# A decoder step on one core: another order and another split of x in the opening

## The chip, the cores and the metric

The kernel runs on one core of a Trainium2 chip. The metric is the device time of one execution in microseconds; the median of three runs stands for a kernel. Engines are named as in the profile: PE is TensorE (PEld its weight loads), ACT ScalarE, DVE VectorE, POOL GpSimd, SP SyncE, which issues most of the transfers.

## The reference

One layer over 1024 prompt tokens and 8 sample tokens, with 1024 features. The part in question is the beginning:

```python
xn = _rmsnorm(h, pre_g)                              # x * rsqrt(mean(x*x) + eps) * gain
proj = jnp.einsum('bld,de->ble', xn, w_in)           # 1024 -> 7168 columns
u, v, z_a, x_b, z_b, g_a, g_b = jnp.split(proj, SPLITS, axis=-1)
...
e = jnp.einsum('blp,pd->bld', p, w_ple)              # embedding, 256 -> 1024, used at the very end
gate = jax.nn.sigmoid(jnp.einsum('bld,de->ble', _rmsnorm(h, ple_in_g), w_pg))
h = h + _rmsnorm(gate * e, ple_out_g)
```

Everything is float32, and the products must be close to float32 in precision.

## The kernel before

**Products.** A float32 operand is split into a high and a low part (`split`: ACT copies to the rounded type `F32R`, DVE subtracts that from the source). A product is three matmuls for each block of 128 features: high by high, high (weights) by low (x), low (weights) by high (x). The normalised x lies in SBUF with features on partitions, in `big`: eight blocks `k` of 128 features, and tokens along the row. `quarter(kp, j)` is the pair of blocks 2kp and 2kp+1 on half `j` of the tokens (512 each; half 1 also has the 8 sample tokens, `[:, :, HALF:]`). B11 and B21 are features 0 to 511 and 512 to 1023 of half 0, B12 and B22 the same of half 1. `xop` holds their high and low parts, as two tiles for each `kp`.

Most products of the kernel use Strassen's seven, on sums (T1 to T4) of these quarters, which are made in place in `big` (`combine`); so `big` must hold the whole values of x. The first pair of v columns goes the plain way (`classical`), with four steps: `steps[0]` is A11 by B11 plus A12 by B21, `steps[1]` A21 by B11 plus A22 by B21, and `steps[2]` and `steps[3]` the same on half 1. Each step's `prepare` splits its weights (128x512 each; `vw`), `run` puts 24 matmuls (48 on half 1) into one PSUM region, `evacuate` copies it out on ACT.

**PSUM.** There are three regions of two banks (`region`) and two single banks (`bank`); each new one takes the place of one that is done with, and PE waits until that has been read.

**Order.** Each engine takes its instructions strictly in the order of its queue. Up to `steps[2]` and the embedding of tile 6, the order on every queue is that of the calls in `begin()`. After that a planner sets the order by estimated times and due times (`Planner.order`), starting from the estimated state at the end of the opening.

**The opening.** `begin()` issues all early loads on SP: p (256 features of the embedding input) and its weights first, then x tiles 0 to 3, the sample rows, the weights of v, x tiles 4 to 7, the second half of p. Until p lands, PE transposes the identity into `warm`. Then:

- `p_turn(h, q)` turns two tiles of p by four transposes and splits them; `we.cut` splits the embedding's weights.
- `embed(t)` multiplies the embedding of token tile t (12 matmuls into a region) and `embed_out` copies it to SBUF (ACT, or DVE for tile 0) and stores it.
- `norm_root(t)` squares x tile t on ACT with a sum, DVE adds epsilon (`ms`), POOL raises to -0.5 (`rstd`); `norm_scale(t)` multiplies the tile on DVE. `S` is the sample's tile `xe`.
- `x_half(j, kps)` turns x: for each `kp` eight transposes of 128x128 into a region (`pst`), copied with the gain to `big` on DVE for even and on ACT for odd `kp`. `x_extra` does it for the sample (eight small transposes `pxe`, four DVE multiplications). `xop.cut` then splits a quarter from `big`.

Before the change, `begin()` has `x_half(0, (0, 1, 2))`, `x_extra`, `xop.cut("B11")`, `x_half(0, (3,))`, `embed(3)`, `xop.cut("B21")` and `steps[0].run()`; the roots of tiles 4 to 7 stand behind that, and half 1 is turned behind `steps[1].run()`, followed by its cuts and `embed(4)`, `embed(5)` and `steps[2].run()`.

Of the kernel before, what the change touches and what calls it, by code (L numbers as in the profile page):

```python
# [12 lines left out]
AF = mybir.ActivationFunctionType  # L13
ALU = mybir.AluOpType
# [291 lines left out]
def hybrid_step(  # L306
# [103 lines left out]
    def quarter(kp, j):  # L410
        both = big[:, 2 * kp : 2 * kp + 2, :].rearrange("p a t -> p (a t)")
        return (both[:, 2 * HALF :] if j else both[:, : 2 * HALF]).rearrange("p (k t) -> p k t", k=2)
# [170 lines left out]
            t = 2 * self.pair + m  # L583
            return big[:, 4 * k : 4 * k + 4, t * P : (t + 1) * P]

    def product(form, ps, weights, operand, what, first, last, again=False):

        plan.apart()
        wide = what not in ("B11", "B21", "T4")
        for k in range(4):  # L590
            (wh, wl), (xh, xl) = weights, operand.at(what, k)
            for i, (w, x) in enumerate(((wh, xh), (wh, xl), (wl, xh))):
                for o, c in form.pieces(ps, wide):
                    nc.tensor.matmul(o, w[:, k, :], x[:, c],
                                     start=first and k == 0 and i == 0, stop=last and k == 3 and i == 2,
                                     skip_group_check=again)

    def halves(t, j):

# [9 lines left out]
    def classical(weights, operand, user):  # L609

        steps, regions = [], {}
        for j in range(2):
            for m in range(2):
                names = [f"A{m + 1}{k + 1}" for k in range(2)]

                def prepare(names=names):
                    for n in names:
                        if n not in weights.ready:
                            weights.prepare(n)

                def run(names=names, j=j, m=m):
                    ps = regions[m, j] = region("acc")
                    for i, n in enumerate(names):
                        product(Features, ps, weights.ready[n], operand, f"B{i + 1}{j + 1}", i == 0, i == 1)

                def evacuate(j=j, m=m):
                    user.direct(m, j, Features.view(regions[m, j], j == 1))

                steps.append(Step(prepare, run, evacuate))
        steps[0].loads = lambda: (weights.fetch(), user.loads())  # L630
        steps[-1].after.append(user.finish)
        return steps
# [194 lines left out]

    col = lambda i, k: gvec[:, i * NB + k : i * NB + k + 1]

    def x_half(j, kps):  # L830

        for kp in kps:
            ps = region("pst")
            for kk in range(2):
                k = 2 * kp + kk
                for i in range(4):
                    nc.tensor.transpose(ps[:, kk, i * P : (i + 1) * P],
                                        xts[4 * j + i][:, k * P : (k + 1) * P], ident)
            out = quarter(kp, j)[:, :, :HALF]
            for kk in range(2):  # L840
                o, i, gain = out[:, kk], ps[:, kk], col(0, 2 * kp + kk)
                if kp % 2:
                    nc.scalar.activation(out=o, in_=i, func=AF.Copy, scale=gain)
                else:
                    nc.vector.tensor_scalar_mul(o, i, gain)

    def x_extra():
        ps = bank("pxe").rearrange("p (k t) -> p k t", k=NB)
# [366 lines left out]
    def pairs_of(c0, cls, key):  # L1215
        return [(Weights(inp(c0, i), key), cls(i, key)) for i in range(NPAIR)]
# [2 lines left out]
        step.after.append(f)  # L1219


    vsteps, vusers = [], []
    for i, (w, u) in enumerate(pairs_of(V0, V, "v")):
        vsteps.append((strassen if i else classical)(w, xop, u))
        vusers.append(u)
    gasteps = [strassen(w, xop, u) for w, u in pairs_of(GA0, Gate, "ga")]
    usteps = []
    zausers = []
# [369 lines left out]

    def embed_terms(t, n, terms):

        if t not in e_ps:
            e_ps[t] = region("e")
        todo = left.setdefault((t, n), 6)
        for k, (i, j) in terms:
            nc.tensor.matmul(e_ps[t][:, n], pcut[t // 4][i][:, k, t % 4 * P : (t % 4 + 1) * P], we.at(n, k)[j],
                             start=todo == 6, stop=todo == 1)
            todo -= 1
        left[t, n] = todo

    def embed(t):  # L1610
        for n in range(2):
            embed_terms(t, n, [(0, HH), (0, HL), (0, LH), (1, HH), (1, HL), (1, LH)])

    def embed_out(t, by=None):
        e = slot("e", (P, 2, HALF))
        if by is None:
            nc.scalar.activation(out=e, in_=e_ps.pop(t), func=AF.Copy)
        else:
            nc.vector.tensor_copy(e, e_ps.pop(t))
        r = t // 2 * 2 * P  # L1620
        dma(kept["e"][r : r + 2 * P].rearrange("(p i) (n c) -> i p n c", i=2, n=2)[t % 2], e)

# [7 lines left out]
    def begin():  # L1630
        psl = slot("psamp", (P, PLE))
        p_load(0, 0)
        for i, v in enumerate((pre_g, pool_scale, ple_in_g)):
            dma(vecs[i * NB : (i + 1) * NB, :], v[0].rearrange("(k p) -> k p", p=P), nc.scalar)
        we.fetch(0)
        p_load(0, 1)
        we.fetch(1)
        for t in range(4):
            x_load(t)
        dma(xe[:NS], x_sample)  # L1640
        steps[0].loads()
        for t in range(4, NB):
            x_load(t)
        for q in range(2):
            p_load(1, q)
        dma(psl[:NS], p_sample)
        praw.append(psl)
        steps[4].loads()
        fetched[0] = 5
        early_loads()  # L1650

        ps = bank("warm")
        for t in range(12):
            nc.tensor.transpose(ps[:, t % 4 * P : (t % 4 + 1) * P], ident, ident)
        p_turn(0, 0)
        we.cut(0, 0)
        we.cut(0, 1)
        ps = bank("warm")
        for t in range(4):
            nc.tensor.transpose(ps[:, t * P : (t + 1) * P], ident, ident)  # L1660
        p_turn(0, 1)
        for k in range(2):
            for t in range(2):
                embed_terms(t, 0, [(k, HH)])
            for t in range(2):
                embed_terms(t, 0, [(k, LH)])
        for t in range(2):
            embed_terms(t, 0, [(0, HL), (1, HL)])
        we.cut(1, 0)
        we.cut(1, 1)  # L1670
        for t in range(2):
            embed_terms(t, 1, [(0, HH), (0, LH), (1, HH), (1, LH), (0, HL), (1, HL)])
        norm_root(0)
        embed_out(0, nc.vector)
        norm_root(1)
        norm_scale(0)
        embed(2)
        norm_root(2)
        norm_scale(1)
        norm_root(3)  # L1680
        norm_scale(2)
        embed_out(1)
        norm_scale(3)
        norm_root(S)
        vps = bank("vecs")
        nc.tensor.transpose(vps[:, : 3 * NB], vecs[: 3 * NB, :], ident[: 3 * NB, : 3 * NB])
        nc.vector.tensor_copy(gvec, vps[:, : 3 * NB])
        embed_out(2)
        norm_scale(S)
        steps[0].prepare()  # L1690
        x_half(0, (0, 1, 2))
        x_extra()
        xop.cut("B11")
        x_half(0, (3,))
        embed(3)
        xop.cut("B21")
        steps[0].run()
        embed_out(3)
        norm_root(4)
        norm_root(5)  # L1700
        norm_scale(4)
        steps[1].prepare()
        norm_scale(5)
        norm_root(6)
        norm_root(7)
        norm_scale(6)
        norm_scale(7)
        steps[0].evacuate()
        steps[1].run()
        x_half(1, (0, 1))  # L1710
        for q in range(2):
            p_turn(1, q)
        x_half(1, (2, 3))
        steps[1].evacuate()
        xop.cut("B12")
        embed(4)
        xop.cut("B22")
        embed_out(4)
        embed(5)
        embed_out(5)  # L1720
        prepared[0] = 4
        steps[2].run()
        steps[2].evacuate()
        embed(6)
        embed_out(6)
# [47 lines left out]
```

## Time and profile before

| | us |
|---|---|
| three runs | 991.76, 990.98, 991.16 |
| their median | 991.16 |
| the profiled execution | 991.0 |
| its span, first to last instruction | 989.3 |

The profile is of one execution. Its page gives the busy time of each engine, and the timeline the start, the length and, in brackets, the idle time ahead of an instruction and what ended it. A PE row's length is modelled; matmuls overlap, so their starts tell the pace. Several equal instructions in a row are one line, with their count.

### The profile page before, as it was taken

Reading aid. Unit: us, or ns where it says so; the run is one execution under the profiler, and the core shown is the slowest. Engines: PE = TensorE matmul, PEld = TensorE weight load, DVE = VectorE, ACT = ScalarE, POOL = GpSimd, SP = SyncE. Lnnn points to the kernel's source line nnn. Section 1 sums busy time; section 2 is a strip of 40 time slices with the busy share of each in tenths; the row PEclk is TensorE's granted clock in tenths of the full one; section 3 lists DMA queues with packets and bytes.
Section 4 is the critical chain, followed back from the end, with each engine's and each line's share of the span. In section 5 each row is a group of like instructions: output and inputs, shape, how many; then the busy total and the mean of one; then the engine's idle time right before and its main releaser. Section 6 shows DMA issues by size and latency. Waiting matters only on the chain. (4 is left out here: it accounts for less than half of the span.)

```text
span 989.3 us, 15945 instructions
## 1 busy us (share of the span) xinstructions
PE 975.0 (99%) x6087; PEld 875.3 (88%) x6087; DVE 797.4 (81%) x1239; ACT 529.6 (54%) x888; POOL 69.9 (7%) x142
## 2 busy tenths in 40 slices
PE   8999999999999999999999999999999999999996
PEld 7789999999998999999999999999999988888885
DVE  6796568787769888979897987697799899779696
ACT  7778987565434433344442333562353365877463
POOL 2100001000000000000000100000000001313111
PEclk9999999999999999999999999999999999999999
DMA  9335553322374354556735075973663552699546
GB/s 339 132 104 117 120 151 128 129 85 75 120 256 149 125 202 142 215 197 213 255 124 191 17 268 207 315 281 131 228 244 124 177 191 63 133 299 361 149 109 191
DMA packets 109291, 174.53 MB, mean 176 GB/s; under 512 B 28632, under 2 KB 68016, under 8 KB 109207
## 3 DMA queue, kind: packets, MB, share of 16 engines
q1 hardware_dynamic: 107118, 166.13, 49.1%
q0 software_dynamic: 2048, 7.37, 4.4%
q8 instruction: 48, 0.79, 0.3%
q14 instruction: 29, 0.23, 0.1%
q10 hardware_dynamic: 48, 0.01, 0.0%
HBM read 114.84 MB, written 53.87 MB: 171 GB/s over the span
## 5 line engine op out<-in xcount | busy, mean ns | idle before, releaser
L299 DVE TENSOR_TENSOR u<-acc,u 128x520 f32<-128x520 f32 (+1 forms) x90 | 62.6, 696 | 37.3 <-PE acc L299 33.5
L299 POOL TENSOR_TENSOR rstd<-ms,mhalf 128x1 f32<-128x1 f32 (+1 forms) x36 | 32.3, 900 | 193.5 <-DVE ms L299 183.8
L299 POOL MEMSET u<- 128x8 f32 x35 | 4.0, 150 | 499.9 <-PE acc L299 235.8
L299 ACT ACTIVATE u<-acc 128x512 f32<-128x512 f32 x39 | 23.2, 595 | 25.6 <-PE acc L299 25.0
L299 ACT ACTIVATE paw<-pas 128x512 fp32r<-128x512 f32 x16 | 10.1, 629 | 30.0 <-DVE pas L299 24.8
L299 ACT ACTIVATE pbw<-pbs 128x512 fp32r<-128x512 f32 x16 | 10.0, 628 | 28.0 <-DVE pbs L299 24.8
L299 DVE TENSOR_TENSOR big<-big 128x1024 f32<-128x1024 f32 (+4 forms) x20 | 23.6, 1218 | 0.0
L299 ACT ACTIVATE big<-mix 128x256 f32<-128x256 f32 x32 | 12.1, 383 | 19.1 <-PE mix L299 16.8
L299 PE MATMUL accm<-qh,wpoolw 128*128 128x260 f32 (+1 forms) x96 | 20.9, 319 | 0.0
L299 ACT ACT_TABLE_LOAD x13 | 16.7, 1283 | 7.2 <-PE acc L299 6.2
L299 ACT ACTIVATE big<-v 128x1024 uint16<-128x1024 uint16 x16 | 18.5, 1175 | 3.8 <-DMA v<-vw 3.8
L299 ACT ACTIVATE zbw<-zbs 128x512 fp32r<-128x512 f32 x16 | 10.1, 628 | 16.7 <-DVE zbs L299 11.8
L299 DVE TENSOR_TENSOR v<-acc,u 128x520 f32<-128x520 f32 (+1 forms) x9 | 6.3, 697 | 15.4 <-PE acc L299 15.4
L299 DVE TENSOR_TENSOR acc<-acc,u 128x512 f32<-128x512 f32 (+1 forms) x16 | 11.2, 699 | 8.7 <-PE acc L299 8.7
L299 ACT ACTIVATE gbw<-gbs 128x512 fp32r<-128x512 f32 x16 | 10.0, 626 | 15.0 <-DVE gbs L299 12.8
L299 ACT ACTIVATE zaw<-zas 128x512 fp32r<-128x512 f32 x16 | 10.0, 630 | 14.6 <-DVE zas L299 9.1
L299 ACT ACTIVATE uw<-us 128x512 fp32r<-128x512 f32 x16 | 10.0, 626 | 13.7 <-DVE us L299 11.1
L299 PEld LDWEIGHTS accm<-qh,wpoolw 128*128 128x128 f32 x96 | 15.6, 188 | 1.9
L299 DVE TENSOR_TENSOR big<-mix,big 128x256 f32<-128x256 f32 x32 | 12.7, 420 | 5.5 <-ACT big L299 5.1
L299 ACT ACTIVATE gb<-gb 128x1032 f32<-128x1032 f32 (+1 forms) x8 | 6.8, 854 | 19.0 <-DVE gb L299 19.0
L299 ACT ACTIVATE vw<-v 128x1024 uint16<-128x1024 uint16 x16 | 16.1, 1046 | 0.5 <-DVE v L299 0.5
L299 ACT ACTIVATE big<-h 128x1024 f32<-128x1024 f32 (+1 forms) x12 | 13.0, 1092 | 5.0 <-DMA h<-in_x_prompt_dram 5.0
(690 smaller groups left out, 3623.5 us busy)
## 6 DMA issues: line engine op xcount, KB each, us to landing
ga<-ga SPq DMA_DIRECT2D x16, 516.0 KB
gb<-gb SPq DMA_DIRECT2D x16, 516.0 KB
ya<-za SPq DMA_DIRECT2D x8, 516.0 KB
yb<-zb SPq DMA_DIRECT2D x8, 516.0 KB
x<-in_x_prompt_dram SPq DMA_DIRECT2D x8, 512.0 KB
vraw<-in_w_in_dram SPq DMA_DIRECT2D x8, 512.0 KB
e<-e SPq DMA_DIRECT2D x8, 512.0 KB
garaw<-in_w_in_dram SPq DMA_DIRECT2D x8, 512.0 KB
```

The source lines that it names most:

```text
L299: getattr(getattr(self.nc, e), method)(*args, **kwargs)
```

## The change

The opening is put in another order, and x is split in another way.

- *Fillers:* seven in place of twelve before p, six in place of four after its first turn. The first four embedding matmuls come ahead of p's second turn.
- *Embedding:* tile 3 is multiplied ahead of x, into two single banks, and copied out by DVE; tile 0's copy by DVE comes after the root of tile 2.
- *The split of x:* for each `kp`, ACT copies the two blocks from PSUM with the gain to the high part, and DVE makes the low part from PSUM, the gain and the high part in one operation. `kp` 3 uses two banks in place of a region. The copy into `big` is made later by POOL, which adds high and low part (`x_whole`); for `kp` 2 and 3 of half 1 ACT copies it from PSUM.
- *The first product* takes the low weights last (`late`).
- *Order:* the weights A11 and A12 are prepared between, the roots of tiles 4 to 6 and of the sample, the sample's turn and both turns of the second half of p now stand between the first and the second product, and half 1 is turned in one piece behind the second.

```diff
-    def product(form, ps, weights, operand, what, first, last, again=False):
+    def product(form, ps, weights, operand, what, first, last, again=False, late=False):
+        order = [(k, i) for k in range(4) for i in range(3)]
+        if late:
+            order.sort(key=lambda x: x[1] == 2)
...
-    def x_half(j, kps):
+    def x_half(j, kp):
+        if kp < NB // 2 - 1:
             ps = region("pst")
+            ps = [ps[:, kk] for kk in range(2)]
+        else:
+            ps = [bank("pst") for _ in range(2)]
+        for kk in range(2):
+            k = 2 * kp + kk
+            for i in range(4):
+                nc.tensor.transpose(ps[kk][:, i * P : (i + 1) * P], xts[4 * j + i][:, k * P : (k + 1) * P], ident)
+        hi, lo = xop.new(f"B{kp // 2 + 1}{j + 1}", kp % 2)
+        for kk in range(2):
+            nc.scalar.activation(out=hi[:, kk, :HALF], in_=ps[kk], func=AF.Copy, scale=col(0, 2 * kp + kk))
+        for kk in range(2):
+            nc.vector.scalar_tensor_tensor(out=lo[:, kk, :HALF], in0=ps[kk], scalar=col(0, 2 * kp + kk),
+                                           in1=f32(hi[:, kk, :HALF]), op0=ALU.mult, op1=ALU.subtract)
+        out = quarter(kp, j)
+        if j:
+            split(out[:, :, HALF:], hi[:, :, HALF:], lo[:, :, HALF:])
+        if j and kp > 1:
             for kk in range(2):
-                k = 2 * kp + kk
-                for i in range(4):
-                    nc.tensor.transpose(ps[:, kk, i * P : (i + 1) * P],
-                                        xts[4 * j + i][:, k * P : (k + 1) * P], ident)
-            out = quarter(kp, j)[:, :, :HALF]
-            for kk in range(2):
-                o, i, gain = out[:, kk], ps[:, kk], col(0, 2 * kp + kk)
-                if kp % 2:
-                    nc.scalar.activation(out=o, in_=i, func=AF.Copy, scale=gain)
-                else:
-                    nc.vector.tensor_scalar_mul(o, i, gain)
+                nc.scalar.activation(out=out[:, kk, :HALF], in_=ps[kk], func=AF.Copy, scale=col(0, 2 * kp + kk))
+
+    def x_whole(j, kp):
+        hi, lo = (f32(x[:, :, :HALF]) for x in xop.parts[f"B{kp // 2 + 1}{j + 1}", kp % 2])
+        nc.gpsimd.tensor_tensor(out=quarter(kp, j)[:, :, :HALF], in0=hi, in1=lo, op=ALU.add)
...
         ps = bank("warm")
-        for t in range(12):
+        for t in range(7):
...
         norm_root(0)
-        embed_out(0, nc.vector)
         norm_root(1)
         norm_scale(0)
-        embed(2)
-        norm_root(2)
-        norm_scale(1)
-        norm_root(3)
-        norm_scale(2)
-        embed_out(1)
-        norm_scale(3)
-        norm_root(S)
         vps = bank("vecs")
         nc.tensor.transpose(vps[:, : 3 * NB], vecs[: 3 * NB, :], ident[: 3 * NB, : 3 * NB])
         nc.vector.tensor_copy(gvec, vps[:, : 3 * NB])
+        embed(2)
+        norm_root(2)
+        embed_out(0, nc.vector)
+        norm_root(3)
+        norm_scale(1)
+        norm_scale(2)
+        embed_out(1)
+        embed(3)
+        norm_scale(3)
         embed_out(2)
+        embed_out(3)
+        vweights[0].prepare("A11")
+        for kp in range(3):
+            x_half(0, kp)
+        vweights[0].prepare("A12")
+        x_half(0, 3)
+        x_whole(0, 0)
+        x_whole(0, 1)
+        steps[0].run()
+        steps[1].prepare()
+        norm_root(4)
+        norm_root(S)
+        norm_scale(4)
+        norm_root(5)
         norm_scale(S)
-        steps[0].prepare()
-        x_half(0, (0, 1, 2))
+        norm_root(6)
+        norm_scale(5)
         x_extra()
-        xop.cut("B11")
-        x_half(0, (3,))
-        embed(3)
-        xop.cut("B21")
-        steps[0].run()
-        embed_out(3)
-        norm_root(4)
-        norm_root(5)
-        norm_scale(4)
-        steps[1].prepare()
-        norm_scale(5)
-        norm_root(6)
+        for q in range(2):
+            p_turn(1, q)
         norm_root(7)
         norm_scale(6)
+        steps[0].evacuate()
         norm_scale(7)
-        steps[0].evacuate()
+        x_whole(0, 2)
+        x_whole(0, 3)
         steps[1].run()
-        x_half(1, (0, 1))
-        for q in range(2):
-            p_turn(1, q)
-        x_half(1, (2, 3))
         steps[1].evacuate()
-        xop.cut("B12")
+        for kp in range(4):
+            x_half(1, kp)
+        x_whole(1, 0)
+        x_whole(1, 1)
         embed(4)
-        xop.cut("B22")
         embed_out(4)
```

## Rows read from the trace of the kernel before

**Rows 1.** The page, busy time of the engines over the span:

```profile
PE 975.0 (99%) x6087; PEld 875.3 (88%) x6087; DVE 797.4 (81%) x1239; ACT 529.6 (54%) x888; POOL 69.9 (7%) x142
```

**Rows 2.** Table by stretch: stretch, length, busy time of each engine, granted clock:

```profile
core 0: us, PE busy (x) PEld busy (x) DVE busy (x) ACT busy (x) POOL busy (x), PEclk, DMA share, GB/s
5.00:6.00 1.00, 1.00 (x7) 0.99 (x5) 0.00 (x0) 0.36 (x1) 0.00 (x0) 1.00 1.00 363
47.00:64.00 17.00, 17.00 (x121) 15.98 (x120) 16.96 (x20) 9.55 (x15) 0.00 (x0) 1.00 0.33 124
64.00:100.00 36.00, 36.00 (x229) 32.18 (x228) 25.38 (x38) 31.67 (x56) 0.00 (x0) 1.00 0.49 116
```

**Rows 3.** List of PE's waits, 90 us to the end: total, times, longest:

```profile
PE acc L299 <- DVE u L299: 0.5, 1, 0.5
```

**Rows 4.** Timeline of PE, 1.9 to 6.9 us: start, length, instructions:

```profile
1.92 2.42 PEld L299 LDWEIGHTS warm<-ident 128*128 128x128 f32 x12 [1.92 <-POOL ident masks.py:199]
...
4.33 0.87 PEld L299 LDWEIGHTS pp<-ident,p 128*128 128x128 f32 x4
...
6.38 0.42 PEld L299 LDWEIGHTS pp<-ident,p 128*128 128x128 f32 x4 [0.40 <-PE warm L299]
6.42 0.63 PE L299 MATMUL pp<-ident,p 128*128 128x128 f32 x4 [0.19 <-DMA p<-in_p_prompt_dram]
...
6.81 0.73 PE L299 MATMUL e<-wehi,ph 128*128 128x512 f32 x2
```

**Rows 5.** Timeline of PE, 16.9 to 47 us, at its waits:

```profile
16.96 2.51 PE L299 MATMUL pst<-ident,x 128*128 128x128 f32 x21 [0.86 <-DVE ms L299]
...
29.52 0.19 PEld L299 LDWEIGHTS acc<-xB11h,vw 128*128 128x128 f32 x1 [0.40 <-ACT vw L299]
...
41.55 0.50 PE L299 MATMUL e<-wehi,ph 128*128 128x512 f32 x1 [1.36 <-ACT big L299]
...
46.99 0.41 PEld L299 LDWEIGHTS acc<-xB12h,vw 128*128 128x128 f32 x2
```

**Rows 6.** Timeline of ACT, 17.5 to 28.9 us:

```profile
17.59 1.13 ACT L299 ACTIVATE vw<-vraw 128x512 fp32r<-128x512 f32 x2
18.64 1.27 ACT L299 ACTIVATE big<-pst,gvec 128x512 f32<-128x512 f32 x2
...
26.76 1.06 ACT L299 ACTIVATE squares<-x 128x1024 f32<-128x1024 f32 x1
...
27.80 1.06 ACT L299 ACTIVATE squares<-x 128x1024 f32<-128x1024 f32 x1
```

**Rows 7.** Groups by operation and shape, whole span: busy us, mean ns of one:

```profile
L299 DVE SCALAR_TENSOR_TENSOR zb<-accm,gvec,zb 128x512 f32<-128x512 f32 x8 | 6.0, 748 | 1.9 <-PE accm L299 1.9
...
L299 POOL MEMSET sst<- 128x1024 f32 x1 | 1.3, 1287 | 0.0
```

**Rows 8.** Timeline around the sample's tile, 17.6 to 22.6 us:

```profile
17.61 0.74 DVE L299 TENSOR_SCALAR xe<-xe,rstd 8x1024 f32<-8x1024 f32 x1 [0.56 <-POOL rstd L299]
...
19.40 0.57 PEld L299 LDWEIGHTS pxe<-ident,xe 8*128 8x128 f32 x8 [0.17 <-issue]
...
22.12 0.40 DVE L299 TENSOR_TENSOR big<-pxe,gvec 128x16 f32<-128x16 f32 x4
```

**Rows 9.** Timeline of POOL and DVE, where both work:

```profile
11.01 0.55 POOL L299 TENSOR_TENSOR rstd<-ms,mhalf 128x1 f32<-128x1 f32 x1 [9.14 <-DVE ms L299]
...
103.45 1.10 POOL L299 TENSOR_SCALAR_AFFINE_SELECT ws<-ws 128x1024 f32<-128x1024 f32 x1 [69.33 <-DMA lnvec<-in_ln_g_dram]
104.02 0.70 DVE L299 TENSOR_TENSOR v<-acc,u 128x520 f32<-128x520 f32 x1 [2.18 <-PE acc L299]
...
150.87 2.13 POOL L299 TENSOR_TENSOR rstd<-ms,mhalf 128x1 f32<-128x1 f32 x1 [8.25 <-DVE ms L299]
...
151.91 0.68 DVE L299 TENSOR_TENSOR gaw<-gas,gaw 128x512 fp32r<-128x512 f32 x1
```

**Rows 10.** Timeline, the low part of T2 and its first matmul:

```profile
62.12 0.25 DVE L299 TENSOR_TENSOR xT2l<-big,xT2h 128x16 fp32r<-128x16 f32 x2
...
69.36 0.40 PE L299 MATMUL acc<-xT2h,vw 128*128 128x260 f32 x2
```

More of the change, by code (lines that the diff above doesn't have):

```diff
@@ L584, in quarter @@
             return big[:, 4 * k : 4 * k + 4, t * P : (t + 1) * P]
-    def product(form, ps, weights, operand, what, first, last, again=False):
+    def product(form, ps, weights, operand, what, first, last, again=False, late=False):
         plan.apart()
         wide = what not in ("B11", "B21", "T4")
-        for k in range(4):
+        order = [(k, i) for k in range(4) for i in range(3)]
+        if late:
+            order.sort(key=lambda x: x[1] == 2)
+        for n, (k, i) in enumerate(order):
             (wh, wl), (xh, xl) = weights, operand.at(what, k)
[L592 to L596, printed above, removed]
+            w, x = ((wh, xh), (wh, xl), (wl, xh))[i]
+            for o, c in form.pieces(ps, wide):
+                nc.tensor.matmul(o, w[:, k, :], x[:, c], start=first and n == 0, stop=last and n == 11,
+                                 skip_group_check=again)
     def halves(t, j):
@@ L623, in run @@
                     for i, n in enumerate(names):
-                        product(Features, ps, weights.ready[n], operand, f"B{i + 1}{j + 1}", i == 0, i == 1)
+                        product(Features, ps, weights.ready[n], operand, f"B{i + 1}{j + 1}", i == 0, i == 1,
+                                late=j == m == 0)
                 def evacuate(j=j, m=m):
@@ L828, in hybrid_step @@
     col = lambda i, k: gvec[:, i * NB + k : i * NB + k + 1]
-    def x_half(j, kps):
-        for kp in kps:
+    def x_half(j, kp):
+        if kp < NB // 2 - 1:
             ps = region("pst")
-            for kk in range(2):
-                k = 2 * kp + kk
-                for i in range(4):
-                    nc.tensor.transpose(ps[:, kk, i * P : (i + 1) * P],
-                                        xts[4 * j + i][:, k * P : (k + 1) * P], ident)
-            out = quarter(kp, j)[:, :, :HALF]
-            for kk in range(2):
-                o, i, gain = out[:, kk], ps[:, kk], col(0, 2 * kp + kk)
-                if kp % 2:
-                    nc.scalar.activation(out=o, in_=i, func=AF.Copy, scale=gain)
-                else:
-                    nc.vector.tensor_scalar_mul(o, i, gain)
+            ps = [ps[:, kk] for kk in range(2)]
[15 more added lines that the diff above has]
+        if j and kp > 1:
+            for kk in range(2):
+                nc.scalar.activation(out=out[:, kk, :HALF], in_=ps[kk], func=AF.Copy, scale=col(0, 2 * kp + kk))
+    def x_whole(j, kp):
+        hi, lo = (f32(x[:, :, :HALF]) for x in xop.parts[f"B{kp // 2 + 1}{j + 1}", kp % 2])
+        nc.gpsimd.tensor_tensor(out=quarter(kp, j)[:, :, :HALF], in0=hi, in1=lo, op=ALU.add)
     def x_extra():
@@ L1219, in at @@
         step.after.append(f)
-    vsteps, vusers = [], []
+    vsteps, vusers, vweights = [], [], []
     for i, (w, u) in enumerate(pairs_of(V0, V, "v")):
@@ L1225, in hybrid_step @@
         vusers.append(u)
+        vweights.append(w)
     gasteps = [strassen(w, xop, u) for w, u in pairs_of(GA0, Gate, "ga")]
@@ L1599, in embed_terms @@
     def embed_terms(t, n, terms):
-        if t not in e_ps:
+        if t == 3:
+            e_ps[t, n] = e_ps.get((t, n)) or bank("e")
+        elif t not in e_ps:
             e_ps[t] = region("e")
+        out = e_ps[t, n] if t == 3 else e_ps[t][:, n]
         todo = left.setdefault((t, n), 6)
         for k, (i, j) in terms:
-            nc.tensor.matmul(e_ps[t][:, n], pcut[t // 4][i][:, k, t % 4 * P : (t % 4 + 1) * P], we.at(n, k)[j],
+            nc.tensor.matmul(out, pcut[t // 4][i][:, k, t % 4 * P : (t % 4 + 1) * P], we.at(n, k)[j],
                              start=todo == 6, stop=todo == 1)
@@ L1615, in embed_out @@
         e = slot("e", (P, 2, HALF))
-        if by is None:
+        if t == 3:
+            for n in range(2):
+                nc.vector.tensor_copy(e[:, n], e_ps.pop((t, n)))
+        elif by is None:
             nc.scalar.activation(out=e, in_=e_ps.pop(t), func=AF.Copy)
         else:
-            nc.vector.tensor_copy(e, e_ps.pop(t))
+            by.tensor_copy(out=e, in_=e_ps.pop(t))
         r = t // 2 * 2 * P
@@ L1658, in begin @@
         ps = bank("warm")
-        for t in range(4):
-            nc.tensor.transpose(ps[:, t * P : (t + 1) * P], ident, ident)
+        for t in range(6):
+            nc.tensor.transpose(ps[:, t % 4 * P : (t % 4 + 1) * P], ident, ident)
+        for i in (HH, LH):
+            for t in range(2):
+                embed_terms(t, 0, [(0, i)])
         p_turn(0, 1)
-        for k in range(2):
+        for i in (HH, LH):
             for t in range(2):
-                embed_terms(t, 0, [(k, HH)])
-            for t in range(2):
-                embed_terms(t, 0, [(k, LH)])
+                embed_terms(t, 0, [(1, i)])
         for t in range(2):
```

## The prediction, made before the changed kernel had run

> **What bounds the kernel now.** I read the page's engine line first: TensorE is busy for 975.0 of 989.3 us [rows 1]. So a change to the opening can pay only where TensorE waits or does filler, and I went to the table by stretch to see up to where that is. From 47 us on it is busy in every microsecond up to 100 us [rows 2], and in the list of waits its longest single one after that is 0.5 us [rows 3]. What counts is therefore one moment: when the first matmul of the third product on half 1 of x (B12) can load its weights, 46.99 us before the change [rows 5]. Its shift is the shift of the end, if nothing behind it wakes up.
>
> Then I walked the timeline of TensorE to that moment. The filler transposes run from 1.92 to 4.33 us, the first real ones start at 4.33, the second turn of p at 6.38 to 6.42, behind 0.19 us of waiting for its transfer, and the embedding matmuls at 6.81 [rows 4]. There is a wait of 0.86 us for the scaled x before the transposes at 16.96, 0.40 us for the weights of the second product, and 1.36 us at 41.55 until ScalarE has emptied the PSUM region that the embedding of tile 4 needs [rows 5]. With short restarts that is some 3.5 us between 6.81 and 46.99. More than that can't be won.
>
> **The change part by part.** TensorE's prices: 24 matmuls of 512 columns fill 41.55 to 46.99, so 5.45 us, and 21 transposes take 2.51 us, so about 0.113 each behind one another [rows 5].
>
> *Filler and first embedding.* Five of the first twelve fillers go, two are added behind the first split. The first tile of p had landed by 4.33 (no wait is shown), and seven fillers at 0.20 end at 3.3 [rows 4]; it lands between these. I take 4.0, because the second p was waited for until 6.4, and keep 3.4 to 4.33. From the first turn to the first embedding matmul it takes 2.48 us [rows 4], so that one starts at 6.5 (5.9 to 6.8). The second turn of p (0.42) now comes behind four matmuls, which hides its landing.
>
> *Tile 3 ahead of x.* The embedding of tile 3 is the same 12 matmuls (2.7 us), moved in front of the transposes of x, into the 0.86 us wait. TensorE: 6.5 + 24 matmuls 5.5 + p and the vectors 0.6 + 24 matmuls 5.5 = 18.1. The last x tile was scaled just before the transposes at 16.96; VectorE now copies tile 0 ahead of that, 0.8 us at most more, so some 17.7: still covered, and it costs nothing unless x lands 0.4 us later. The 32 transposes (3.6) end at 21.7, the first product (5.5) at 27.2, if its operands keep up. Before, it ended at 29.1: 1.9 us won so far, 0.6 of it owed to the sample's transposes, which now come later.
>
> *The split from PSUM.* What goes: the copies out of PSUM, then an ACT and a DVE split of the copy. What comes, for each group of two blocks: two ACT copies with the gain (0.59 from start to start, like ACT's copies with a gain) and two DVE operations that read PSUM and one SBUF tile (0.75 each: the nearest row is the same operation on PSUM, a column and an SBUF tile) [rows 6, 7]. ACT sees the first group at 18.1 + 0.9 + 0.25 = 19.25, and its eight copies take 4.7. DVE follows one behind, so the last low part stands at 25.9 with the low part of A12 in between. The product, reordered so that the low weights come last, needs that at about 26, so it loses some 0.3 at most.
>
> *The sample's turn becomes a wait.* On TensorE's queue the sample's transposes and the two turns of p now stand between the first and the second product. They need the scaled sample. On ACT, behind the eight copies (23.95), come A12, A21 and A22 (1.6, by two in 1.13), then the squares of tile 4, of the sample and of tile 5, at 1.04 each [rows 6]: 25.6, 27.8, 28.8. On DVE the sample's scaling stands behind the root of tile 5: 28.9 + 0.74 [rows 8] = 29.65. TensorE, ready at 27.3, waits 2.4 us, with the whole second product queued behind. Then eight transposes (0.57), and the second turn of p needs the PSUM bank of the sample, which DVE frees only after the scaling of tile 5 (squares of tile 6 at 29.9, 30.75) and its four multiplications (0.40) [rows 8]: 31.2, plus one turn 0.45. The second product runs from 31.7 to 37.2, the other 32 transposes to 40.8, and the embedding of tile 4 starts there, since its PSUM region was read a microsecond earlier. That is **0.8 us ahead** of 41.55, with nothing charged for GpSimd.
>
> *GpSimd adds up the whole values.* Six additions of 128x1024 floats; the trace has none on GpSimd. Its bounds: one pass over such a tile with one input took 1.10 us [rows 9], a fill 1.29 [rows 7]; two inputs as two such passes are 2.2, and with the 0.55 of a 128x1 operation of the same kind [rows 9] 2.75. I take 2.2, as this reads two tiles, and keep 1.1 to 2.75. The Trainium skill, GPSIMD Engine Reference, section "Elementwise — side-by-side cycle accounting", gives 4497 ns for such an addition of 2048 elements; half of it, an estimate, is 2.25 us, which would leave the sum as it is.
>
> The price is in what stands beside them. While DVE ran operations with two SBUF inputs, the last of them until 152.6, a root on GpSimd that started at 150.87 and takes 0.55 alone took 2.13 us, until they were done; while GpSimd passed over 128x1024 (103.45 to 104.55), a DVE operation that read PSUM and one SBUF tile took its usual 0.70 at 104.02 [rows 9]. So the two exclude each other when DVE needs two SBUF inputs, and the new low parts of x, which read PSUM, are free of it. That DVE waits when GpSimd came first, no row shows. The Trainium skill says so: SBUF — State Buffer, section "Who interferes with whom": a DVE instruction with two SBUF inputs, or a fast one-input copy, and a GpSimd instruction that reads SBUF hold the same ports for the whole instruction, and the later one blocks. By that rule the time is my forecast's; without it, that of the first rival.
>
> If DVE waits: the first addition runs 21.5 to 23.7 (behind the first group's low part), the second 23.7 to 25.9. DVE asks for the low part of A12 (two SBUF inputs) at 23.9 and waits until 25.9: 2.0 us, with the last group's low parts, A21, A22 and the roots queued behind it. The first product then ends at 29.0, and the sample is scaled at 31.65, so the second product comes 2.0 later as well. A second time: behind the root of tile 7 GpSimd's next addition starts just as DVE wants to scale tile 7, which costs 0 or 2.2 us at DVE, of which TensorE sees 0.9; I take 0.7. The additions themselves are wanted only by the sums T1 to T4; the low part of T2 was ready at 62.4 for a matmul at 69.36 [rows 10], so they have seven microseconds.
>
> **Sum.** -0.8 + 2.0 + 0.7 = +1.9 us on the profiled execution's 991.0: **992.9 us**. That execution lies 0.16 below the median of the three runs, 991.16, within their spread.
>
> **The rivals.**
> *A, GpSimd costs DVE nothing* (DVE isn't held, or the additions take 1.1 and are through at 23.9): 991.0 - 0.8 = **990.2**. For it: no row shows DVE held. Against it: the exclusion itself.
> *B, TensorE's clock rises late: slower.* The fillers and the first turn took 0.20 each until 6.0 and the next ones 0.105 at 6.38 [rows 4]: the step from 1.2 to 2.4 GHz in durations, although the granted clock reads 1.00 between 5 and 6 us too [rows 2]; before it TensorE had worked from 1.92 without a gap. Now it stands still from 3.3 to about 4.0. Each microsecond by which the rise comes into the embedding matmuls costs half a microsecond: nothing if it comes by 6.5 as before, 5.5 us if all of the first 24 run at the lower level. I take 1.5, a rise 3 us into them, as the pause is short. All of it reaches x, which ACT is waiting for. It decides if the embedding matmuls still stand 0.46 apart at 7 us. Middle: +3.4 on the forecast, **994.4**; on A 991.7.
> *C, the split isn't what it says:* the low parts, whose column and high part are both in SBUF, are held by the additions too. Each of the two then delays a group by 2.2: 4.4 more than A instead of 2.0, **about 995**. Against it: the 0.70 at 104.02.
> *D,* the order of all later work is worked out anew from estimates, and tile slots may come free in another order: within a microsecond either way.
>
> **How the numbers follow.** Forecast 0.50, A 0.28, B 0.12, C 0.05, D 0.05. A measurement of this kernel can tell 0.2% (2.0 us) from no change. The forecast's size follows the addition's length (some 0.7 at 1.5 us, 2.9 at 2.75), so it is slower with 0.23 and no change with 0.27; A is no change but for 0.04; B is slower with 0.07; C all; D is spread. Faster 0.06, same 0.57, slower 0.37. Eight in ten lie between 990.0 (A with an early p) and 995.0 (B on the forecast); the forecast alone spans 991.7 to 994.
>
> **What would show it.** Embedding matmuls from about 6.5, 0.23 apart; the transposes of x without a wait at 18; the first product's end at 27 (A) or 29; the wait for the sample's scaling, over 2 us, whichever it is; DVE's low part of A12 starting at the end of a GpSimd addition; additions of about 2.2 us. I am wrong if the sample is scaled before the first product ends (then up to 2.5 us are won), or if TensorE waits behind 47 us.

## The result, and the profile after

| | before | after |
|---|---|---|
| median of six runs, us | 991.19 | 994.85 |
| their range | 990.98 to 992.5 | 993.99 to 996.04 |
| the profiled execution | 991.0 | 994.45 |
| its span | 989.3 | 992.7 |

The ratio of after to before is 1.0032, with a 95% interval of 1.0022 to 1.0043: the change costs about 3.7 us, where 1.9 had been forecast. The time lies in the range given.

The page's line answers to [rows 1]. TensorE is busy 1.0 us longer with three fillers fewer, and GpSimd 15.7 us longer, of which the six additions are 15.4.

```profile
PE 976.0 (98%) x6084; PEld 875.3 (88%) x6084; DVE 799.8 (81%) x1245; ACT 528.4 (53%) x895; POOL 85.6 (9%) x148
```

The list of TensorE's waits from 0 to 50 us, and behind it the one from 50 us to the end (total, times, longest), answers to [rows 3, 5]:

```profile
PE pxe L299 <- DVE ms L299: 3.0, 1, 3.0
...
PE acc L299 <- DVE u L299: 1.2, 1, 1.2
```

The waits of the old opening (0.86, 0.40 and 1.36 us) are gone, and one wait of 3.0 us for the scaled sample has taken their place. The timeline of TensorE and of its weight loads (PEld) shows where it stands, to compare with [rows 4, 5]:

```profile
3.53 0.72 PEld L299 LDWEIGHTS pp<-ident,p 128*128 128x128 f32 x4 [0.25 <-DMA p<-in_p_prompt_dram]
...
6.40 0.73 PE L299 MATMUL e<-wehi,ph 128*128 128x512 f32 x2 [0.47 <-ACT wehi L299]
...
18.44 3.66 PE L299 MATMUL pst<-ident,x 128*128 128x128 f32 x32
...
22.38 0.47 PE L299 MATMUL acc<-xB11h,vw 128*128 128x512 f32 x1 [0.28 <-DVE xB11l L299]
...
31.31 0.63 PE L299 MATMUL pxe<-ident,xe 8*128 8x8 f32 x8 [3.04 <-DVE ms L299]
...
33.15 0.25 PEld L299 LDWEIGHTS acc<-xB11h,vw 128*128 128x128 f32 x1
...
40.16 0.91 PEld L299 LDWEIGHTS pst<-ident,x 128*128 128x128 f32 x7
...
44.31 0.47 PE L299 MATMUL e<-wehi,ph 128*128 128x512 f32 x1 [0.28 <-DVE xB12l L299]
...
49.73 0.42 PEld L299 LDWEIGHTS acc<-xB12h,vw 128*128 128x128 f32 x2
```

The first product runs from 22.3 to 28.3. Then TensorE stands still until the sample has been scaled. The second product takes from 33.15 to 40.16, 7.0 us for 24 matmuls that take 5.45 elsewhere [rows 5]. The table by stretch says why (stretch, length, busy time of PE, PEld, DVE, ACT, POOL, granted clock, DMA share, GB/s):

```profile
31.00:33.00 2.00, 1.42 (x14) 1.22 (x15) 1.31 (x7) 0.38 (x1) 1.40 (x2) 1.00 0.47 193
33.00:34.00 1.00, 1.00 (x6) 0.90 (x5) 0.69 (x1) 0.70 (x2) 0.00 (x0) 0.61 0.01 4
34.00:35.00 1.00, 1.00 (x4) 0.71 (x4) 0.69 (x1) 1.00 (x3) 0.00 (x0) 0.50 0.00 0
35.00:36.00 1.00, 1.00 (x4) 0.81 (x3) 0.81 (x2) 0.65 (x3) 0.51 (x1) 0.50 0.00 0
36.00:37.00 1.00, 1.00 (x5) 0.78 (x4) 0.56 (x2) 0.00 (x0) 1.00 (x2) 0.68 0.02 8
37.00:38.00 1.00, 1.00 (x6) 0.82 (x5) 1.00 (x1) 0.00 (x0) 1.00 (x1) 1.00 0.00 0
```

After the pause the granted clock falls to 0.50, the lower of its two levels (1.2 of 2.4 GHz), while TensorE is busy in every microsecond; it is back at 1.00 from 37 us. The price is 7.0 less 5.45, or 1.6 us.

The timelines of DVE and of POOL in the same stretch:

```profile
20.82 2.73 DVE L299 SCALAR_TENSOR_TENSOR xB11l<-pst,gvec,xB11h 128x512 fp32r<-128x512 f32 x4 [0.89 <-ACT xB11h L299]
23.46 1.40 DVE L299 SCALAR_TENSOR_TENSOR xB21l<-pst,gvec,xB21h 128x512 fp32r<-128x512 f32 x2
24.78 0.68 DVE L299 TENSOR_TENSOR vw<-vraw,vw 128x512 fp32r<-128x512 f32 x1
25.38 1.41 DVE L299 SCALAR_TENSOR_TENSOR xB21l<-pst,gvec,xB21h 128x512 fp32r<-128x512 f32 x2
26.69 2.19 DVE L299 TENSOR_TENSOR vw<-vraw,vw 128x512 fp32r<-128x512 f32 x2
...
30.43 0.74 DVE L299 TENSOR_SCALAR xe<-xe,rstd 8x1024 f32<-8x1024 f32 x1
...
36.46 2.88 DVE L299 TENSOR_SCALAR x<-x,rstd 128x1024 f32<-128x1024 f32 x1 [0.44 <-POOL rstd L299]
...
45.48 1.29 DVE L299 TENSOR_TENSOR xB12l<-big,xB12h 128x16 fp32r<-128x16 f32 x1
```

```profile
22.37 5.36 POOL L299 TENSOR_TENSOR big<-xB11h,xB11l 128x1024 f32<-128x1024 f32 x2 [6.46 <-DVE xB11l L299]
...
36.40 5.23 POOL L299 TENSOR_TENSOR big<-xB21h,xB21l 128x1024 f32<-128x1024 f32 x2
...
44.31 4.79 POOL L299 TENSOR_TENSOR big<-xB12h,xB12l 128x1024 f32<-128x1024 f32 x2 [2.69 <-DVE xB12l L299]
```

The three rows of POOL hold two additions each. Taken one by one, four of the six take 2.39 to 2.43 us. The other two, the second of the first pair (from 24.74) and the second of the next (from 38.75), take 3.00 and 2.88: the low part of A12 and the scaling of tile 7 run on DVE in their first 0.6 to 0.7 us, so there GpSimd is the one held. DVE is held in four places: at the low part of A21 (2.19 for A21 and A22, which take 0.68 each alone), at the scaling of tile 7 (2.88 against 0.75), and at two small remainders beside the last pair, the sample's columns of x (1.29 at 45.48 and 1.12 at 48.02, where the same 128x16 operation takes 0.17 at 44.08).

**Where the 3.45 us of the two profiled executions lie.** B12's weights load 2.74 us later (49.73 against 46.99). The matmuls that follow keep this shift up to 65 us; behind the sample's state (69.36 before) it has become 3.05, behind the wait for u (320.36 before) 3.9, and the end is 3.45 later.

### The profile page after: what moved, and what is told of

The parts are those of the page before. It is cut to its first block, busy times and chain, and to the rows that moved or that the text cites. A ratio compares the mean times of both kernels' runs of the same rounds, so it can differ in the third digit from the quotient of the medians.

```text
span 992.7 us, 15977 instructions
## 1 busy us (share of the span) xinstructions
PE 976.0 (98%) x6084; PEld 875.3 (88%) x6084; DVE 799.8 (81%) x1245; ACT 528.4 (53%) x895; POOL 85.6 (9%) x148
## 5 line engine op out<-in xcount | busy, mean ns | idle before, releaser
L299 ACT ACTIVATE big<-mix 128x256 f32<-128x256 f32 x32 | 12.1, 384 | 19.0 <-PE mix L299 16.7
L299 ACT ACT_TABLE_LOAD x13 | 16.7, 1283 | 7.1 <-PE acc L299 6.1
L299 PE MATMUL mix<-wst,vh 128*128 128x256 f32 x64 | 15.6, 319 | 0.0
```

What stands on the lines that cost most here:

```text
L299: getattr(getattr(self.nc, e), method)(*args, **kwargs)
```

## The experiments

After the comparison the theory was: the opening loses what the sample's place costs, by the wait and, through the pause, by the clock (theory 1). Its rival: GpSimd's additions, by holding DVE, cost the time, and the sample only shows it. All ratios are to the kernel before, run beside each.

**1. The sample's and p's turns behind the second product.**

```diff
         norm_scale(5)
-        x_extra()
-        for q in range(2):
-            p_turn(1, q)
         norm_root(7)
...
         steps[1].evacuate()
+        x_extra()
+        for q in range(2):
+            p_turn(1, q)
```

> The sample's turn and both turns of the second half of p stand behind the second product instead of in front of it; nothing else is changed against the changed kernel. Theory 1 (the wait of 3.04 us for the sample's scaling, and the fall of TensorE's clock to 0.50 behind it, carry the loss): no wait between the first and the second product, granted clock 1.00 throughout, B12's first weights at about 44.7 instead of 49.7 us, 989 to 991 us. Rival (GpSimd's additions, which hold DVE, carry it): the hold only moves on to the scaling of tile 7 and the time stays at 993 to 994.5.

Measured: 992.8 us (991.79 to 994.29, ten runs), ratio 1.0014 (1.0004 to 1.0023). In the profiled execution the wait between the products is gone, and the granted clock is 1.00 in every microsecond from 26 to 50. But the gain is smaller than expected: B12's weights load at 47.29 instead of 44.7. In this execution x is split 0.6 us later than in the changed kernel's, and a new wait stands behind the second product. TensorE's timeline, then DVE's:

```profile
37.50 0.63 PE L299 MATMUL pp<-ident,p 128*128 128x128 f32 x4 [1.91 <-issue]
...
41.89 0.47 PE L299 MATMUL e<-wehi,ph 128*128 128x512 f32 x1 [0.28 <-DVE xB12l L299]
```

```profile
34.23 2.84 DVE L299 TENSOR_SCALAR x<-x,rstd 128x1024 f32<-128x1024 f32 x1 [0.44 <-POOL rstd L299]
36.99 0.40 DVE L299 TENSOR_TENSOR big<-pxe,gvec 128x16 f32<-128x16 f32 x4
```

The second turn of p needs the sample's bank of PSUM, which DVE frees by four multiplications at 36.99; these are queued behind the scaling of tile 7, held 2.1 us by the addition that started at 34.17. So both theories have a share: the sample's place costs the larger part of the loss (the ratio falls from 1.0032 to 1.0014), and with it out of the way the hold on tile 7, hidden before, comes to the path.

**2. Only the clock: 25 filler transposes in the wait.** Everything else stays as in the changed kernel.

```diff
         norm_scale(5)
+        ps = bank("warm")
+        for t in range(25):
+            nc.tensor.transpose(ps[:, t % 4 * P : (t % 4 + 1) * P], ident, ident)
         x_extra()
```

> 25 transposes of the identity are put between the first product and the sample's turn, into TensorE's wait of 3 us; they compute nothing that is used. Theory 1: the wait remains as filler, the granted clock stays at 1.00 in the second product, its 24 matmuls take 5.5 instead of 7.2 us, and the time falls by 1.4 to 1.8 to about 993.2. Rival (the slow stretch is not owed to the pause, but to contention there): no change, 994.5 to 995.

Measured: 992.65 us (991.76 to 993.37, ten runs), ratio 1.0009 (1.0000 to 1.0019). TensorE's timeline, and the table by stretch:

```profile
28.00 2.89 PE L299 MATMUL warm<-ident 128*128 128x128 f32 x25
31.22 0.63 PE L299 MATMUL pxe<-ident,xe 8*128 8x8 f32 x8 [0.33 <-DVE ms L299]
...
42.90 0.47 PE L299 MATMUL e<-wehi,ph 128*128 128x512 f32 x1 [0.27 <-DVE xB12l L299]
```

```profile
34.00:35.00 1.00, 1.00 (x6) 0.80 (x5) 0.68 (x1) 1.00 (x3) 0.00 (x0) 1.00 0.28 115
35.00:36.00 1.00, 1.00 (x6) 0.82 (x5) 0.84 (x2) 0.48 (x1) 0.68 (x1) 1.00 0.02 8
```

The sample comes at the same time (31.22 against 31.31), the clock stays at 1.00, and tile 4's embedding starts 1.4 us earlier. This is the clean test of the clock: the sample comes when it came before the edit, work without use was added, and the kernel is faster, with an interval below that of the changed kernel. The mean granted clock, listed for each run, is 0.994 to 0.996 in the six runs of the changed kernel and 0.997 to 0.998 in the ten of this one, so the fall is most likely not that of the profiled execution alone (the mean also takes in the end of the span). Of the 1.6 us, 0.29 comes back as a wait for tile 7's scaling. The end is 2.0 us earlier in the profiled execution, more than at tile 4, as the wait for u is 0.66 in place of 1.16.

**3. Only the hold on A21: the first two additions later.** They move behind the scaling of tile 5, past the low parts of A21 and A22 and the first roots.

```diff
-        x_whole(0, 0)
-        x_whole(0, 1)
         steps[0].run()
...
         norm_scale(5)
+        x_whole(0, 0)
+        x_whole(0, 1)
         x_extra()
```

> GpSimd's first two additions are issued behind the scaling of tile 5 instead of ahead of the first product; the sample's turn stays where it is. Theory 1: DVE's low part of A21 is not held (0.68 instead of 1.59 us), the sample is scaled about 0.9 us earlier and TensorE waits 2.2 instead of 3.04 us: 994.0 if the clock falls all the same, 992.4 if the shorter pause leaves it. Rival (the hold carries the loss): 991 to 992.

Measured: 994.24 us (993.93 to 996.33, eight runs), ratio 1.0029 (1.0019 to 1.0040): no difference from the changed kernel that can be told, and near the 994.0 that theory 1 gave for a clock that falls all the same. DVE's, then TensorE's timeline, and the table by stretch:

```profile
26.89 1.29 DVE L299 TENSOR_TENSOR vw<-vraw,vw 128x512 fp32r<-128x512 f32 x2
```

```profile
30.61 0.63 PE L299 MATMUL pxe<-ident,xe 8*128 8x8 f32 x8 [2.14 <-DVE ms L299]
...
40.17 3.38 PE L299 MATMUL pst<-ident,x 128*128 128x128 f32 x29 [0.39 <-DVE x L299]
```

```profile
32.00:33.00 1.00, 1.00 (x7) 0.94 (x6) 0.00 (x0) 0.60 (x1) 1.00 (x1) 0.50 0.51 209
```

The low parts of A21 and A22 take 1.29 where they took 2.19: the additions had held them, by 0.9 us. The sample is there 0.7 earlier. But a pause of 2.14 us is followed by the same fall of the clock, and the additions, now later, delay the root and the scaling of tile 7 until TensorE waits for it. Taking GpSimd's hold from this place alone wins nothing.

**4. Both: the sample late and all additions late.** To experiment 1's edit, the first two additions move behind the scaling of tile 7.

```diff
-        x_whole(0, 0)
-        x_whole(0, 1)
         steps[0].run()
...
         norm_scale(7)
+        x_whole(0, 0)
+        x_whole(0, 1)
         x_whole(0, 2)
```

> The sample's turn as in e1_sample_late, and GpSimd's first two additions behind the scaling of tile 7, with the other two of half 0. Theory 1: within 0.7 us of e1_sample_late, since the roots are then no longer what TensorE waits for. Rival: another 2 us better than e1_sample_late.

Measured: 993.69 us (992.36 to 996.36, ten runs), ratio 1.0026 (1.0015 to 1.0037), not better than experiment 1. TensorE's, then DVE's timeline:

```profile
35.74 0.63 PE L299 MATMUL pp<-ident,p 128*128 128x128 f32 x4 [1.04 <-issue]
40.14 0.47 PE L299 MATMUL e<-wehi,ph 128*128 128x512 f32 x1 [0.27 <-DVE xB12l L299]
43.77 0.47 PE L299 MATMUL e<-wehi,ph 128*128 128x512 f32 x1 [0.63 <-DVE xB12l L299]
47.34 0.51 PE L299 MATMUL acc<-xB12h,vw 128*128 128x260 f32 x2 [0.58 <-ACT big L299]
```

```profile
39.91 2.39 DVE L299 TENSOR_TENSOR xB12l<-big,xB12h 128x16 fp32r<-128x16 f32 x1
```

Tile 4's embedding starts 1.75 us ahead of experiment 1's. Half of that, 0.88, is there before the edit can act, as x is split that much earlier in this execution; the rest is p's shorter wait (1.04 in place of 1.91). All but 0.06 of it is lost again at 47.93, a few matmuls into the third product (47.99 in experiment 1): GpSimd now adds without a break from 32.4 to 47, beside the low parts of half 1, whose small remainders, the sample's columns taken from SBUF, are held (2.39 us for a 128x16 subtraction that takes 0.17 alone). Neither theory had this: the later place for the additions wins 0.87 at 40 and costs 1.7 at 44 and 47. No place tried in this stretch was free for all six on GpSimd.

**5. The opening's fillers as they were.** Twelve and four in place of seven and six.

```diff
-        for t in range(7):
+        for t in range(12):
...
-        for t in range(6):
+        for t in range(4):
```

> The changed kernel with the fillers of the kernel before: twelve ahead of p and four behind its first turn, in place of seven and six; nothing else. In the changed kernel's profiled runs TensorE pauses for 0.25 to 0.5 us ahead of p, and in some of them the first embedding matmuls stand 0.38 apart until 7.4 to 7.9 us instead of 0.23. Theory 1 (the pause lets the clock rise later, by an amount that changes from run to run): p's first turn starts at 4.33, the embedding at 6.8, always at 0.23, the runs spread less than the changed kernel's 2.05 us, and the time is between 0.6 us lower and 0.3 us higher, 994.3 to 995.1. Rival (the fillers don't matter, the transfers do): same spread, and 0.3 to 0.4 us higher, as the embedding starts later.

Measured: 995.35 us (994.99 to 996.06, six runs), ratio 1.0035 (1.0022 to 1.0047): the same as the changed kernel. TensorE's timeline and the table by stretch:

```profile
6.80 1.21 PE L299 MATMUL e<-wehi,ph 128*128 128x512 f32 x2 [0.35 <-ACT wehi L299]
```

```profile
32.00:38.00 6.00, 5.81 (x24) 5.14 (x25) 3.47 (x11) 2.72 (x5) 2.20 (x4) 0.50 0.09 35
```

The embedding starts 0.4 later, as before the change [rows 4], and its first matmuls still stand 0.5 apart in this execution, so the fillers don't secure the rise of the clock. The runs spread over 1.1 us in place of 2.05, as theory 1 had it, but lie 0.5 higher, nearer to the rival. After the wait for the sample (3.05 us) the lower level lasted over six microseconds here, in place of some three and a half. How long it lasts after the same pause is not the same in each execution; what decides that stays open.

**6. Two additions by VectorE.** Experiment 1's edit; and kp 2 and 3 of half 0 are added by DVE behind the turns of p, not by GpSimd ahead of the second product.

```diff
-        x_whole(0, 2)
-        x_whole(0, 3)
         steps[1].run()
         steps[1].evacuate()
+        x_extra()
+        for q in range(2):
+            p_turn(1, q)
+        for kp in (2, 3):
+            x_whole(0, kp, nc.vector)
```

> As e1_sample_late, but the additions for kp 2 and 3 of half 0 are made by DVE behind the sample's multiplications, so that GpSimd can't hold the scaling of tile 7. Theory 1 (in e1_sample_late that hold, 2.84 instead of 0.75 us for the scaling, moved TensorE's wait to the second turn of p): no wait over 0.5 us up to the third product, B12's first weights 1.5 to 2 us earlier than in e1_sample_late (47.3), 990.5 to 991.5, level with the kernel before or better. Rival (DVE's own additions, 1.22 each, delay the low parts of half 1 as much): as e1_sample_late, 992.5 to 993.

Measured: 991.25 us (990.8 to 994.68, eleven runs), ratio 1.0000 (0.9991 to 1.0009). With nothing on GpSimd at 34, tile 7 is scaled in 0.75 us, p's turn doesn't wait, and experiment 1's wait of 1.91 us is gone. So the addition's hold on tile 7 was behind that wait, and is the second part of the loss; the intervals of the two experiments just overlap, so this rests on the trace more than on the times. DVE adds in 1.2 us what takes GpSimd 2.4 alone. The time is the one expected, the path isn't: B12's weights load at 46.38, 0.9 ahead of experiment 1, where 1.5 to 2 had been expected, because the delay that the rival had named came too. DVE's, then TensorE's timeline show it:

```profile
37.16 2.35 DVE L299 TENSOR_TENSOR big<-xB21h,xB21l 128x1024 f32<-128x1024 f32 x2
39.43 1.40 DVE L299 SCALAR_TENSOR_TENSOR xB12l<-pst,gvec,xB12h 128x512 fp32r<-128x512 f32 x2
```

```profile
40.98 0.47 PE L299 MATMUL e<-wehi,ph 128*128 128x512 f32 x1 [1.66 <-DVE xB12l L299]
```

**7. The same with the old fillers.** Experiment 6 with experiment 5's edit.

> e6_adds_on_dve with the fillers of the kernel before (twelve and four). Theory 1: between 0.6 us lower and 0.3 us higher than e6_adds_on_dve, and a smaller spread; if the late rise of the clock costs most runs half a microsecond or more, this is the fastest and below the kernel before. Rival: 0.3 to 0.4 us above e6_adds_on_dve.

Measured: 991.04 us (990.54 to 991.82, eleven runs), ratio 0.9993 (0.9984 to 1.0001). The median hardly moves, and the wait of 1.66 us at 41 stays. The runs lie within 1.3 us, where those of experiment 6 spread over 3.9; that the fillers did this isn't shown, since the profiled executions of experiments 5 and 8 have a late rise with them too.

**8. The two additions of VectorE in its gaps.** Experiment 7, with one addition behind the sample's multiplications and one behind kp 2 of half 1.

```diff
         x_extra()
+        x_whole(0, 2, nc.vector)
         for q in range(2):
             p_turn(1, q)
-        for kp in (2, 3):
-            x_whole(0, kp, nc.vector)
         for kp in range(4):
             x_half(1, kp)
+            if kp == 2:
+                x_whole(0, 3, nc.vector)
```

> The additions of the two late pairs of half 0, made by VectorE in the variant before in one piece ahead of half 1's low parts (2.35 us, and TensorE then waited 1.66 us at 41.13 for the first of these), stand in two gaps of VectorE instead: one behind the sample's four multiplications, where VectorE waited 0.86 us for the high part of p, the other behind the low part of the third pair of half 1, where it waited 0.88 us. If the wait at 41 was the price of these two operations alone, the embedding of tile 4 starts at about 39.5 and the third product's weights on half 1 load at about 44.9: 1.7 us less than the variant before, 989.3 in all (0.998 of the kernel before). Rival: ScalarE's copies of half 1 set that moment (the first high parts were there at 38.15, so the low part can't end before 39.5 or 39.6, but the region of PSUM may be read by more than that), or the low part of p, now 0.3 us later, holds the embedding: then the wait shrinks by less than half, and the time stays at 990.3 or more. A gain that is given back behind 47 us (a wait for u at 320, 0.5 us before the change and 1.1 in the variant) would show as an early third product and a time still at 990.3.

Measured: 990.59 us (989.97 to 991.46, eleven runs), ratio 0.9986 (0.9977 to 0.9995): the only version whose interval lies below the kernel before. TensorE's timeline, and its waits from 47 us on:

```profile
40.18 0.48 PE L299 MATMUL e<-wehi,ph 128*128 128x512 f32 x1 [0.27 <-DVE xB12l L299]
```

```profile
PE acc L299 <- DVE u L299: 1.0, 1, 1.0
...
PE sps L299 <- DVE sst L299: 0.2, 1, 0.2
```

The wait went, as the theory said, and B12's weights load at 45.62, 1.37 us ahead of the kernel before (1.7 ahead of the variant before had been expected; it is 0.94, as the opening of this execution was 0.45 later and tile 4 starts 0.27 after the low part). But the end is only 0.35 ahead in these two executions (by the medians of the runs beside each other, 1.2): 0.45 goes at the sample's state and 0.5 at u, the two places where the changed kernel loses too. The third outcome of the expectation, an early third product and a time above 990.3, is what came.

## Why the prediction was right in direction and range, and short by half

**Right.** TensorE's shift at B12 set most of the end: 2.74 of the 3.45 us are there at 49.73. Fillers and embedding: p was there at 3.5 (4.0 taken, 3.4 to 4.33 given), the first embedding matmul came at 6.40 (6.5), though by two errors that cancel: with p half a microsecond early, the embedding waited 0.47 for the high part of its weights. Tile 3 ahead of x: the transposes of x start at 18.44 without a wait (18.1), and x was scaled by 16.7. The low part from PSUM isn't held by the additions: the last two pairs take 1.40 and 1.41 beside them, so rival C is out. The sample's turn as a wait: forecast 2.4 us without the hold and 2.65 with it, measured 3.04, and the time at which the sample is ready (31.65 forecast) was 31.2. Rival A, no hold on DVE, is out by 2.19, 2.88 and experiment 3. The Trainium skill's page SBUF — State Buffer, section "Who interferes with whom", on whose rule the forecast had leaned without a row for it, is borne out by these: operations of DVE with two SBUF inputs (the low part of A21) and a one-input one (the scaling of tile 7) were held, each by an addition that had started earlier.

**In the range by luck.** The forecast alone spanned 991.7 to 994, and the measured 994.85 lies above that. The range reached 995.0 for the sake of rival B, a late rise of the clock in the first embedding matmuls, and in the profiled execution that rise wasn't late. By the 0.2% that the prediction itself takes as what a measurement can tell, the outcome is slower, to which it had given 0.37, and not no change, at 0.57.

**Mis-sized: the first hold.** The forecast had the low part of A12 held for 2.0 us. It came at 24.78, just as the first addition was through (24.79), and took 0.68. The sign that the prediction had named for the hold, A12's low part starting at the end of an addition, thus appeared without one. The second addition, whose row starts at 24.74, was the one that waited there (3.00 us in place of 2.4), and it then held A21's low part for 0.9. The first addition took 2.42 (2.2 taken) and began later (22.37 against 21.5), because DVE's low part of a pair starts only when ScalarE has made the high part of both its blocks (0.89 us of waiting at 20.82). So the hold was real, but what it costs hangs on which instruction meets it, and that on a few tenths.

**Mis-sized: the second hold.** Tile 7's scaling was held 2.1 us, as forecast (2.2). Of the 0.7 put down for TensorE nothing showed, since the second product itself was late. Experiment 2, without the fall of the clock, shows 0.29 of it, and experiment 1, where the sample's multiplications stand behind it, 1.9.

**Missing: the clock behind the pause.** The step that failed is the sample's turn. The prediction saw the wait and its length, and gave it only its own price. That a pause costs TensorE's clock, it had considered at the opening (rival B) and not here. Price: 1.6 us in the second product; by experiment 2 it is 1.4 at tile 4's embedding (44.31 against 42.90) and 2.0 at the end of the profiled executions. By the ratios (1.0032 and 1.0009) it is the larger part of the whole loss.

**The sum once more, to tile 4's embedding** (43.5 by the forecast, 44.31 measured). The second product starts 0.55 earlier than forecast (33.15 against 33.7), takes 1.5 more than the 5.5 allowed for it, and tile 7 costs nothing (0.7 less). From its end to the embedding it takes 4.15 us, where 3.6 were forecast, as 0.2 goes before the transposes and 0.28 for the low part of B12. Together 0.8.

**Mis-sized: behind 47 us.** "If nothing behind it wakes up": 0.3 at the sample's state and 0.65 at u (1.16 against 0.51 in the timelines) did, 0.2 came between them, and 0.45 came back later. The prediction had named a wait behind 47 us as a sign of being wrong, and rival D had it within a microsecond either way. Experiment 8 loses 0.45 and 0.5 at the same two places with B12 ahead of the kernel before, so it isn't the lateness of the opening that does it. At the sample's state the timelines say a little more: DVE begins the sums T1 to T4 at 51.41 (47.59 before), 3.8 us later where TensorE is 2.74 later, and in experiment 8 at 47.45, 0.14 earlier where TensorE is 1.37 earlier. In both, DVE has fallen behind TensorE by 1.1 to 1.2 us. The held remainders (1.29 and 1.12) stand just ahead of these sums in the changed kernel; that they are the cause wasn't tested by a run, and what makes u late stays open.

Rival B at the opening came true in part: in the profiled executions of experiments 1, 3 and 6, and with the old fillers in those of 5 and 8, the first two embedding matmuls stand 0.5 us apart; in those of the changed kernel and of experiments 2, 4 and 7 they don't. The low parts of x then start later, by 0.2 to 0.6 us in experiments 1, 3 and 6 (against the changed kernel's) and by 0.44 in experiment 8 (against experiment 7's). Comparisons of single executions at this scale have to take that off first. (The rival's time of 994.4 is 3.4 on the 991.0 of before, or 1.5 on the forecast.)

## What to carry to other kernels

Price a new wait of TensorE twice: its own length, and the work behind it at the lower clock (here 3.04 and 1.6 us); the cheapest cure here was filler that has no use (experiment 2, about 0.2% of the whole). Before work goes to an engine with time to spare, ask which other engine it holds up: here one addition on GpSimd cost VectorE up to 2.1 us, where VectorE adds the same in 1.2. And an instruction that waits for the slowest chain, as the sample's did, belongs behind the work that doesn't need it (experiment 1).

## What had not been expected of the hardware

- The granted clock fell to 0.50 after a pause of 3.04 us (changed kernel) and of 2.14 us (experiment 3), and not after the 1.91 us of experiment 1's profiled execution. In other runs of experiment 1 it may have fallen: their mean granted clock is 0.995 to 0.997. At the lower level it stayed some 3.5 us, and in experiment 5 over 6, with TensorE busy for nearly all of that. In the changed kernel and in experiment 3 the pause itself still reads 1.00, and the fall shows when TensorE is at work again; in experiment 5 it begins within the pause (0.89 from 31 to 32 us).
- With 25 filler transposes of the identity in the wait, the clock stayed at 1.00 (experiment 2).
- GpSimd's addition of two 128x1024 tiles took 2.39 to 2.43 us in the changed kernel where DVE didn't hold it. By the Trainium skill, GPSIMD Engine Reference, section "Elementwise — side-by-side cycle accounting", the estimate was 2.25; the measured ones are 6 to 8% above it.
- The same tile scaled by DVE took 0.75 us alone and 2.84 to 2.88 beside an addition that had started up to 0.07 us earlier: it lost 2.1 us, of the 2.4 that the addition ran. The hold works the other way too: an addition behind A12's low part or behind the scaling took 3.00 and 2.88.
